# The last row norms of a hybrid encoder block: ScalarE's order up to tile 6 of the last down products is left to the scheduler, and one small tile grows to 128 bytes

## The chip, the core and the metric

The kernel runs on one core of a Trainium2 chip (trn2). The metric is device time in microseconds, the median of several executions. Times inside a profile are counted from the start of the profiled execution's span.

## What is computed

One encoder layer for 1024 frames of width 1024, all in float32. Only the last lines matter for the change, and the shape of what runs before them:

```python
h = rmsnorm(x, norm1_g)
qkv = h @ w_in                                  # 1024 x 3072
mixed = concat(rmsnorm(chunked_attention(...), norm_a_g),
               rmsnorm(stick_breaking_attention(...), norm_b_g))
x = x + mixed @ w_out
x = x + conv_gated_mlp(rmsnorm(x, norm2_g), ...)  # 1024 -> 2 x 2816 -> conv3 -> SiLU gate -> 1024
return rmsnorm(x, final_g)

def rmsnorm(x, g):
    y = x * rsqrt(mean(x * x, axis=-1) + 1e-6)
    return y * g
```

The end of the kernel computes the last part of the down projection (2816 to 1024), the residual sum, and the final norm of each frame.

## The kernel before

Data lies transposed: a tile has 128 of the 1024 features on its partitions and the 1024 frames along its free dimension, so the output is eight such tiles, here called tile 0 to tile 7 (`d` in the code). A float32 product is made of three products of rounded halves (`high` and `low` of both operands), so each product in the code is three matmuls.

The down projection takes most of the last 200 us. Twenty of the 22 blocks of 128 hidden features go through a scheme with seven products per block pair (L2391). The last two blocks are left to `last_down` (L2251), which is the kernel's end. It cuts the 1024 frames into three pieces, `LAST = ((0, 3), (3, 6), (6, 8))` in units of 128 frames, so 384, 384 and 256 frames. For each piece it goes over the eight tiles:

- TensorE forms tile d's product in six matmuls (`dnl`, L2313).
- VectorE adds it to the sum so far (L2318; into `x2n`, and for the last piece into `res`).
- ScalarE squares the result (`x2_part`, L1679 to L1689): tile 0 goes straight into an accumulator `n_acc` (L1683), the other squares into one of two buffers `n_sq` (L1688), from which GpSimd adds them into the accumulator (L1689). The last tile of the second piece and the last three of the third have accumulators of their own.
- In the last piece, and for the tiles that GpSimd will scale, ScalarE also multiplies by the norm's gain (`gain`, L2298, and L2325).

When a piece's tiles are through, `final` norms it: TensorE sums the accumulators over the partitions (`n_ms`, small matmuls, L171), ScalarE takes the square root (L163) and VectorE the reciprocal (L164), TensorE spreads the result over the partitions by transposes (`n_rb`, L184), ScalarE copies that to `n_rbs` (L2275), VectorE (L2289) and GpSimd (L2287) scale the tiles, and SP sends them out (L2292; L2280 and L2281 for the last piece). The norm of a piece is worked into the tile loop of the piece behind it (`go`): totals behind tile 2's product, transposes behind tile 3's, then a scaling between the adds. On TensorE this order is fixed for the whole kernel. So TensorE reaches the transposes of piece one after tile 3 of piece two, and must wait there if the root and the reciprocal are not done.

Before the first root, ScalarE has to load the table that holds it (ACT_TABLE_LOAD, also L163).

Who sets the order: each engine runs its queue in order. Inside a `tc.manual_schedule(engines=...)` an engine's instructions stand in the order in which the code writes them; outside it a scheduler places them at build time by its own estimate of when operands are ready. Before, `last_down` as a whole runs under a manual order for VectorE, ScalarE and GpSimd; TensorE has one throughout, and SP's order in `last_down` is left to the scheduler.

The second place that the change touches is at the kernel's start. `all_v` (L283) asks for a tile `ms` of 16 float32 values a partition, 64 bytes, for sums of squares. Tiles of a pool lie one behind another, and behind this one lies the place of the tag `c`, used by `v_c` in `all_v` and later by `a22l`, the low half of one operand in the key and query projections, which TensorE streams in the products of L1257.

Of the kernel before, what the change touches and what calls it, by code (L numbers as in the profile page):

```python
# [9 lines left out]
F32 = mybir.dt.float32  # L10
# [6 lines left out]
P = 128  # L17
T = 1024
D = 1024
KT = 8  # L20
# [47 lines left out]
def tile_hybrid_block(  # L68
# [14 lines left out]
    V, S, PE, GP = nc.vector, nc.scalar, nc.tensor, nc.gpsimd  # L83
# [20 lines left out]
    def zbank(name):  # L104
        return pools["psum"].tile([P, GW], F32, tag="z", name=name, bufs=4)
# [14 lines left out]
    def c1(off):  # L120
        t, off = (cst, off) if off < C_W0 else (taps["t"], off - C_W0)
        return t[:, off : off + 1]
# [36 lines left out]
    def cols(k):  # L159
        return slice(k * P, (k + 1) * P)  # L160
# [16 lines left out]
    def rstd(sums, c0, c1, width, rn, name):  # L177

        root(rn[:, c0:c1], totals(sums, c1 - c0, name), width)

    def across(ob, rn, c0, c1):

        for c in range(c0, c1):
            PE.transpose(ob[:, cols(c - c0)], rn[:, c : c + 1].to_broadcast([P, P]), ident)  # L184
# [14 lines left out]
    with tc.tile_pool(name="kp", bufs=2) as kp:  # L199
# [48 lines left out]
        def all_v():  # L248
# [9 lines left out]
            def area(*tiles):  # L258
                return [t[:, r] for t in tiles for r in halves]

            def own(tag, dt=F32R, shape=(P, T)):
                return pools["sbuf"].tile(list(shape), dt, tag=tag, name=f"v_{tag}", bufs=1)
# [17 lines left out]
            ]  # L280
            t4_low = []
            row = area(kp.tile([P, D], F32, tag="rb", name="row", bufs=1))
            ms = own("ms", F32, (P, 2 * KT))  # L283

            def bring(t, src, r):
                nc.sync.dma_start(t[:, r], src[:, r])
# [464 lines left out]
        flow, raw_chains = Flow(), {}  # L751
        S.preload_act_table_set("sqrt_and_others")
        right = all_v()

        fs = Ring(3)
# [397 lines left out]
        shares, pts, x2, yh, yl, yb_of, yq_of, bias_of = {}, {}, {}, {}, {}, {}, {}, {}  # L1153
# [322 lines left out]
        with stage("b"):  # L1476
# [10 lines left out]
            ending = []  # L1487
            for b in range(len(items) + 3):
# [15 lines left out]
                if ending:  # L1504
                    pair, ending = ending, []
# [21 lines left out]
                if 0 <= b - 2 < len(items):  # L1527
# [3 lines left out]
                    if (b - 2) % 4 == 3:  # L1531
                        ending = units[k & ~1 : (k | 1) + 1]
# [62 lines left out]
        for b in range(len(blocks) + 2):  # L1595
            cur = blocks[b] if b < len(blocks) else None
            turning = blocks[b - 1] if 0 <= b - 1 < len(blocks) else None
            ending = blocks[b - 2] if 0 <= b - 2 < len(blocks) else None
# [80 lines left out]
        def x2_part(x2, d, r, accs, pool, name, sq=None):  # L1679

            own = KT - len(accs)
            if d == 0 or d > own:
                S.activation(accs[max(d - own, 0)], x2[d][:, r], AF.Square)  # L1683
            else:
                if sq is None:
                    sq = pool.tile([P, GW], F32, tag="sq", name=f"{name}_sq{d}", bufs=1)
                sq = sq[:, : r.stop - r.start]
                S.activation(sq, x2[d][:, r], AF.Square)  # L1688
                GP.tensor_tensor(out=accs[0], in0=accs[0], in1=sq, op=ALU.add)  # L1689
# [67 lines left out]
    with stage("ffn"):  # L1757
# [3 lines left out]
        def at(slot, name, dt=F32):  # L1761
            pool = wp if slot == "wr" else fp if slot[0] == "s" else cp
            return pool.tile([P, T], dt, tag=slot, name=name, bufs=1)
# [418 lines left out]
        dn_p, x2n, u2n, bank = {}, [None] * KT, [], {}  # L2182
# [57 lines left out]
        NP = 10  # L2240
# [7 lines left out]
                last_w[f] = [at(where[3 + n, k], f"lw{f}_{k}", F32R) for k in (2, 3)]  # L2248
                late.append(lambda f=f: split(*last_w[f], last_raw[f][0]))

        def last_down(chunk, x2):  # L2251
            accs = [
                at(where[1 + i // 2, 2 + i % 2], f"n3_acc{i}") for i in range(4)
            ]
            res = [
                at(where[7, i], f"res{i}").rearrange("p (d t) -> p d t", d=4) for i in range(2)
            ]
            sqs = [at(where[8, i], f"n3_sq{i}") for i in range(2)]

            def final(c0, c_end):  # L2260
                sl = slice(c0 * P, c_end * P)
                last = accs[: {3: 1, 6: 2, 8: 4}[c_end]]
                if c_end == KT:
                    gain(4)
                    gain(5)
                rstd([a[:, sl] for a in last], c0, c_end, D, rn2, f"n3_{c0}")
                if c_end == KT:
                    gain(6)
                    gain(7)
                yield  # L2270
                n = (c_end - c0) * P
                ob = zbank(f"n3_{c0}_rb")[:, :n]
                across(ob, rn2, c0, c_end)
                rb = fp.tile([P, GW], F32, tag="eb", name=f"n3_{c0}_rbs", bufs=1)[:, :n]
                S.copy(rb, ob)  # L2275
                if c_end == KT:
                    for a, g in ENDS:
                        y = res[a // 4][:, a % 4 : a % 4 + 2, :]
                        f = (rb if g else ob).rearrange("p (o t) -> p o t", o=1).to_broadcast([P, 2, n])
                        (GP if g else V).tensor_tensor(out=y, in0=y, in1=f, op=ALU.mult)  # L2280
                        nc.sync.dma_start(outT[a : a + 2, :, sl].rearrange("d p t -> p d t"), y)  # L2281
                    return
                pool_d = POOL_D[c_end]
                for d in range(KT) if c_end == 6 else sorted(range(KT), key=lambda d: d not in pool_d):
                    x = y = x2[d][:, sl]
                    if d in pool_d:
                        GP.tensor_tensor(out=y, in0=x, in1=rb, op=ALU.mult)  # L2287
                    else:
                        V.scalar_tensor_tensor(  # L2289
                            out=y, in0=x, scalar=c1(C_GF + d), in1=ob, op0=ALU.mult, op1=ALU.mult  # L2290
                        )
                    nc.sync.dma_start(outT[d][:, sl], y)  # L2292
                    if d not in pool_d:
                        yield

            def gain(d):
                y = res[d // 4][:, d % 4, :]
                S.activation(y, y, AF.Copy, scale=c1(C_GF + d))  # L2298

            def go(steps):  # L2300
                for _ in range(steps):
                    while todo and next(todo[0], 1):
                        todo.pop(0)

            todo = []
            for c0, c_end in LAST:
                sl = slice(c0 * P, c_end * P)
                for d in range(KT):
                    o = (med if d % 2 else pj)(f"dnl_{d}_{c0}")[:, : (c_end - c0) * P]
                    for n, f in enumerate(chunk):  # L2310
                        (wh, wl), (xh, xl) = last_w[f], last_x[f]
                        for i, (w, t) in enumerate(((wh, xh), (wh, xl), (wl, xh))):
                            PE.matmul(  # L2313
                                o, w[:, cols(d)], t[:, sl], start=n == 0 and i == 0,
                                stop=n == len(chunk) - 1 and i == 2,
                            )
                    y = x2[d][:, sl] if c_end < KT else res[d // 4][:, d % 4, :]
                    V.tensor_tensor(out=y, in0=x2[d][:, sl], in1=o, op=ALU.add)  # L2318
                    last = accs[: {3: 1, 6: 2, 8: 4}[c_end]]
                    x2_part({d: y}, d, slice(0, y.shape[1]), [a[:, sl] for a in last], None, f"n3_{c0}", sqs[d % 2][:, :GW])  # L2320
                    if c_end == KT:
                        if d < 4:
                            gain(d)
                    elif d in POOL_D[c_end]:
                        S.activation(x2[d][:, sl], x2[d][:, sl], AF.Copy, scale=c1(C_GF + d))  # L2325
                    if c_end < KT:
                        go((d > 1) + 2 * (d == KT - 1))
                    elif d in (2, 3, 4):
                        go(1)
                todo.append(final(c0, c_end))  # L2330
            go(3)
            next(todo[-1])
            go(20)
# [74 lines left out]
            do()  # L2408
        own_order.__exit__(None, None, None)
        loads_order.__exit__(None, None, None)  # L2410
        with tc.manual_schedule(engines={V.engine, S.engine, GP.engine}):
            last_down([2 * NP, 2 * NP + 1], x2n)
    pe_order.__exit__(None, None, None)


# [61 lines left out]
```

## Time and profile before

| | |
|---|---|
| median of 3 runs | 1212.38 us (1211.32 to 1212.62) |
| the profiled execution's own time | 1212.13 us |
| its span | 1210.4 us |
| TensorE (PE) busy | 1189.5 us, 98% |
| VectorE (DVE) busy | 925.2 us, 76% |
| ScalarE (ACT) busy | 685.6 us, 57% |
| GpSimd (POOL) busy | 159.9 us, 13% |
| `last_down` begins on TensorE (first dnl matmul) | 1170.8 us |
| last dnl matmul ends | 1200.8 us |
| mean granted TensorE clock | 0.996 |

PE is TensorE's matmuls, PEld its weight loads, DVE VectorE, ACT ScalarE, POOL GpSimd, SP the engine that issues the transfers. A row of instructions gives start, duration, engine, source line, operation, output and inputs, shapes and count, and in brackets the engine's idle time before it with what ended that wait. A row in which several instructions are merged gives the time from the first one's start to the last one's end. A matmul's row lasts longer than the distance to the next, since matmuls overlap. A row of stages gives the stretch, its length, each engine's busy time with the number of instructions that touch it, the granted share of TensorE's clock, the share of the DMA engines' time and GB/s.

### The profile page before, as it was taken

What the parts mean: (1) busy time and instruction counts of PE and PEld (TensorE: products, weight loads), DVE (VectorE), ACT (ScalarE), POOL (GpSimd) and SP (SyncE); (2) the same over time, 40 slices, a digit from 0 to 9 for tenths busy, and PEclk for the clock granted to TensorE, in tenths of its full rate; (3) what the DMA queues carried; (4) which work ended last, traced back from release to release, by engine and by line L of the source; (5) the groups of instructions that cost most, each with busy time, mean ns of one, the idle gap of its engine ahead of it and who ended that gap; (6) DMA issues with size and microseconds to landing.
All of it is one profiled execution on the core that took longest, in us unless ns stands there. A gap on an engine that the chain in (4) does not pass through costs nothing.

```text
span 1210.4 us, 17073 instructions
## 1 busy us (share of the span) xinstructions
PE 1189.5 (98%) x6268; PEld 986.1 (81%) x6268; DVE 925.2 (76%) x1382; ACT 685.6 (57%) x1252; POOL 159.9 (13%) x161
## 2 busy tenths in 40 slices
PE   9999999999999999999999999999999999999996
PEld 7788888888878778788888888888888888888886
DVE  7957749888666767469997776877777779879885
ACT  7865336766667667334766555555555545444425
POOL 0001031102210111331000000000000013133044
PEclk9999999999999999999999999999999999999998
DMA  9467677777468831143122213222231294510003
GB/s 332 134 212 260 193 243 190 214 182 200 140 176 271 215 107 53 37 155 107 53 105 88 89 69 105 70 87 87 70 105 68 91 389 200 214 65 1 1 1 139
DMA packets 73793, 166.92 MB, mean 138 GB/s; under 512 B 7783, under 2 KB 23271, under 8 KB 73710
## 3 DMA queue, kind: packets, MB, share of 16 engines
q1 hardware_dynamic: 73566, 165.79, 42.7%
q8 instruction: 49, 0.80, 0.3%
q14 instruction: 34, 0.28, 0.1%
q10 hardware_dynamic: 144, 0.05, 0.0%
HBM read 118.60 MB, written 47.20 MB: 137 GB/s over the span
## 4 chain that ended last, share of the span: by engine, by line
PE 87%; DVE 7%; ACT 3%; DMA 1%; issue 1%; SPq 1%; DVEq 0%; ACTq 0%
PE u_a L1877 9%; PE u_c L1877 9%; PE u_e L1877 9%; PE dz L2391 8%; PE u_b L1877 5%; PE dj L2391 4%; PE dm L2391 4%; PE pa L154 3%; PE pb L154 3%; PE v_x L508 3%; PE k_p L154 3%; PE yb L1013 3%; PE tpb L999 3%; PE q_p L154 3%; PE yy L1146 2%; PE v_y L508 2%
## 5 line engine op out<-in xcount | busy, mean ns | idle before, releaser
L972 DVE TENSOR_TENSOR_SCAN acts<-zb,first 128x128 f32<-128x128 f32 (+7 forms) x64 | 86.5, 1351 | 18.4 <-ACT zb L981 18.4
L1901 DVE SCALAR_TENSOR_TENSOR vt<-cv,taps,vt 128x1023 f32<-128x1023 f32 (+1 forms) x44 | 58.2, 1323 | 3.3 <-ACT vt L1895 2.5
L1901 DVE SCALAR_TENSOR_TENSOR gt<-cg,taps,gt 128x1023 f32<-128x1023 f32 (+1 forms) x44 | 56.5, 1285 | 1.6 <-ACT gt L1895 0.8
L132 POOL TENSOR_TENSOR dx_0wl<-dr,dx_0wh 128x512 fp32r<-128x512 f32 x1 | 1.4, 1370 | 412.3 <-ACT dx_0wh L2144 412.3
L981 ACT ACTIVATE zb<-zb 128x128 f32<-128x128 f32 (+7 forms) x64 | 41.0, 640 | 26.3 <-PE zb L964 26.3
L1091 ACT ACTIVATE pa<-sa,sta 128x640 f32<-128x640 f32 (+4 forms) x64 | 42.7, 668 | 18.0 <-DVE sta L1082 14.6
L1895 ACT ACTIVATE gt<-cg,cst,taps 128x1024 f32<-128x1024 f32 x22 | 27.4, 1244 | 35.9 <-DVE cg L1769 35.8
L1003 ACT COPY tb<-tpb 128x128 f32<-128x128 f32 (+3 forms) x96 | 43.0, 484 | 6.1 <-PE tpb L999 5.4
L1127 ACT COPY pta<-tpa 128x512 f32<-128x512 f32 (+3 forms) x80 | 36.9, 483 | 13.3 <-PE tpa L1123 13.1
L999 PE MATMUL tpb<-ident,acts 128*128 128x128 f32 x288 | 43.2, 277 | 0.0
L1082 DVE TENSOR_REDUCE sta<-sa 128x1 f32<-128x640 f32 (+4 forms) x64 | 41.8, 655 | 1.3
L1766 DVE TENSOR_TENSOR up_r<-up_r 128x512 f32<-128x512 f32 x60 | 41.3, 688 | 0.8
L1123 PE MATMUL tpa<-ident,pa 128*128 128x128 f32 x240 | 37.9, 277 | 1.1 <-ACT pta L1127 1.1
L999 PEld LDWEIGHTS tpb<-ident,acts 128*128 128x128 f32 x288 | 33.1, 140 | 6.3 <-issue 2.6
L1079 DVE TENSOR_TENSOR sa<-sa,bias 128x256 f32<-128x256 f32 (+1 forms) x64 | 26.4, 414 | 11.0 <-PE sa L1064 7.8
L1123 PEld LDWEIGHTS tpa<-ident,pa 128*128 128x128 f32 x240 | 27.9, 140 | 8.0 <-issue 2.6
L2065 ACT COPY u_b<-u_a 128x512 f32<-128x512 f32 x19 | 10.8, 571 | 38.1 <-PE u_a L1877 38.1
L1146 PE MATMUL yy<-pta,v 128*64 128x256 f32 (+1 forms) x288 | 29.7, 349 | 0.0
L1013 PE MATMUL yb<-tb,dv 128*64 128x128 f32 x448 | 29.2, 273 | 0.0
L154 PE MATMUL pb<-yh,wo_h 128*128 128x512 f32 x64 | 26.9, 421 | 1.8 <-DVE x L1221 1.8
L1689 POOL TENSOR_TENSOR n_acc<-n_acc,n_sq 128x384 f32<-128x384 f32 (+2 forms) x23 | 24.4, 1060 | 29.7 <-ACT n_sq L1688 28.8
L154 PE MATMUL k_p<-hTh,k_h 128*128 128x512 f32 x64 | 27.6, 432 | 0.0
(1400 smaller groups left out, 4004.9 us busy)
## 6 DMA issues: line engine op xcount, KB each, us to landing
up_r<-in_w_up_dram SPq DMA_DIRECT2D x44, 512.0 KB, 3.5
act<-vt SPq DMA_DIRECT2D x22, 512.0 KB, 2.6
dr<-in_w_dn_dram SPq DMA_DIRECT2D x20, 512.0 KB, 7.4
dr<-act SPq DMA_DIRECT2D x20, 512.0 KB, 8.2
wv<-in_w_v_dram SPq DMA_DIRECT2D x16, 256.0 KB, 5.4
xin<-in_xT_dram SPq DMA_DIRECT2D x16, 256.0 KB, 5.4
row<-in_x_rows_dram SPq DMA_DIRECT2D x16, 256.0 KB, 2.6
raw<-in_w_in_dram SPq DMA_DIRECT2D x8, 512.0 KB, 5.3
```

Source lines behind the costliest of these rows:

```text
L154: PE.matmul(o, w[:, sl], t[:, rows(g)], start=first and i == 0, stop=last and i == 2,)
L508: PE.matmul(bank[j], t[:, cols(j)], w, start=p in (1, 5) and k == 0 and i == 0, stop=k == 3 and i == 2, skip_group_check=True,)
L972: V.tensor_tensor_scan(out=a[:, :w], data0=z, data1=first[:, :w], initial=1.0, op0=ALU.mult, op1=ALU.max,)
L999: PE.transpose(tp[:, cols(b)], self.a[h][:, cols(b0 + b)], ident)
L1003: mine.append(flow.add(on_s(m * P, lambda o=o, tp=tp: S.copy(o, tp))))
L1013: PE.matmul(yy[HS[h], :], (d if j else v)[:, off : off + 64], self.at[h][:, self.c0[h] + j * P : self.c0[h] + (j + 1) * P], start=j == 0, ...
L1091: on_s(w + 170, lambda: S.activation(po, full, AF.Exp, bias=st[:, h : h + 1], accum_out=st[:, 2 + h : 3 + h])),
L1123: PE.transpose(tp[:, cols(b)], self.pr[src][:, cols(c)], ident)
L1146: PE.matmul(yy[HS[h], q], v[:, c * P + h * 64 : c * P + (h + 1) * 64], t[:, h], start=j == 0, stop=j == len(parts) - 1, skip_group_check=True,
L1877: PE.matmul(o, w[:, cols(k)], t, start=start and k == 0 and i == 0, stop=k == 3 and i == 2, skip_group_check=True,)
L1901: V.scalar_tensor_tensor(out=t[:, : T - lag], in0=o[:, lag:], scalar=c1(c + ct), in1=t[:, : T - lag], op0=ALU.mult, op1=ALU.add,)
L2391: PE.matmul(o[m], w[:, cols(m)], t, start=i in (0, 1, 4, 5) and p == ps_[0] and j == 0, stop=p == ps_[-1] and j == 2, skip_group_check=True,)
```

## The change

`last_down` gets an `ExitStack`. The manual order is entered at its start for VectorE and GpSimd alone, and for ScalarE only at tile 5 of the last piece, just behind that tile's products. Up to there ScalarE's place for each instruction is the scheduler's choice; from there to the end the code's order holds again. TensorE's, VectorE's and GpSimd's written order is the same. The tile `ms` is asked for with 32 values, 128 bytes, of which the same 16 are used.

```diff
-            ms = own("ms", F32, (P, 2 * KT))
+            ms = own("ms", F32, (P, 4 * KT))[:, : 2 * KT]
...
-        def last_down(chunk, x2):
+        def last_down(chunk, x2, ending):
...
+                    if (c_end, d) == (KT, 5):
+                        ending.enter_context(tc.manual_schedule(engines={S.engine}))
                     y = x2[d][:, sl] if c_end < KT else res[d // 4][:, d % 4, :]
                     V.tensor_tensor(out=y, in0=x2[d][:, sl], in1=o, op=ALU.add)
...
-        with tc.manual_schedule(engines={V.engine, S.engine, GP.engine}):
-            last_down([2 * NP, 2 * NP + 1], x2n)
+        with ExitStack() as ending:
+            ending.enter_context(tc.manual_schedule(engines={V.engine, GP.engine}))
+            last_down([2 * NP, 2 * NP + 1], x2n, ending)
```

In the built program the tiles of tag `c` (two `v_c` and four `a22l`) lie 64 bytes further on than before, at a multiple of 128 bytes; no other tile has another address. No instruction is added or taken away, and the order on TensorE, VectorE and GpSimd is unchanged.

ScalarE around the first root, as a piece of the difference (`n3_sq0` and `n3_sq1` are the two square buffers, `x2n2` is tile 2, `n3_0` the first piece's norm):

```order
 L1688 ACTIVATE n3_sq1_10654<-x2n1_9065 128x384
-L1688 ACTIVATE n3_sq0_10653<-x2n2_9066 128x384
 L163 ACT_TABLE_LOAD
 L163 ACTIVATE rn2_78<-n3_0_ms_10764,eps_75 128x3
+L1688 ACTIVATE n3_sq0_10653<-x2n2_9066 128x384
+L2275 COPY n3_0_rbs_10784<-n3_0_rb_10780 128x384
 L1688 ACTIVATE n3_sq1_10654<-x2n3_9067 128x384
-L2275 COPY n3_0_rbs_10784<-n3_0_rb_10780 128x384
 L1688 ACTIVATE n3_sq0_10653<-x2n4_9068 128x384
```

The square of tile 2 moved behind the table load and the root, and the copy of the spread norm moved ahead of the square of tile 3.

ScalarE around the second root (`res0` holds tiles 0 to 3 of the last piece, `n3_3` is the second piece's norm; L2298 are the gains). Before:

```order
L1683 ACTIVATE n3_acc0_10647<-res0_10651 128x256
L2298 ACTIVATE res0_10651<-res0_10651,cst_66 128x256
L1688 ACTIVATE n3_sq1_10654<-res0_10651 128x256
L2298 ACTIVATE res0_10651<-res0_10651,cst_66 128x256
L1688 ACTIVATE n3_sq0_10653<-res0_10651 128x256
L2298 ACTIVATE res0_10651<-res0_10651,cst_66 128x256
L163 ACTIVATE rn2_78<-n3_3_ms_10875,eps_75 128x3
L1688 ACTIVATE n3_sq1_10654<-res0_10651 128x256
L2298 ACTIVATE res0_10651<-res0_10651,cst_66 128x256
L2275 COPY n3_3_rbs_10899<-n3_3_rb_10895 128x384
```

and now:

```order
L1683 ACTIVATE n3_acc0_10647<-res0_10651 128x256
L1688 ACTIVATE n3_sq1_10654<-res0_10651 128x256
L2298 ACTIVATE res0_10651<-res0_10651,cst_66 128x256
L1688 ACTIVATE n3_sq0_10653<-res0_10651 128x256
L2298 ACTIVATE res0_10651<-res0_10651,cst_66 128x256
L163 ACTIVATE rn2_78<-n3_3_ms_10875,eps_75 128x3
L2298 ACTIVATE res0_10651<-res0_10651,cst_66 128x256
L1688 ACTIVATE n3_sq1_10654<-res0_10651 128x256
L2275 COPY n3_3_rbs_10899<-n3_3_rb_10895 128x384
L2298 ACTIVATE res0_10651<-res0_10651,cst_66 128x256
```

Of the gains of tiles 0 to 3 each stands one place later among the squares, so that two of them instead of three stand ahead of the root, and the copy moved ahead of the last of them.

SP's output transfers of the second piece, whose order the scheduler sets:

```order
 L2292 DMA out_0_dram<-x2n1_9065 128x384
+L2292 DMA out_0_dram<-x2n2_9066 128x384
 L2292 DMA out_0_dram<-x2n6_9070 128x384
-L2292 DMA out_0_dram<-x2n7_9071 128x384
-L2292 DMA out_0_dram<-x2n2_9066 128x384
 L2292 DMA out_0_dram<-x2n3_9067 128x384
 L2292 DMA out_0_dram<-x2n4_9068 128x384
+L2292 DMA out_0_dram<-x2n7_9071 128x384
 L2292 DMA out_0_dram<-x2n5_9069 128x384
```

Tiles 6 and 7, which GpSimd scales, moved back behind tiles that VectorE scales; in the first piece tile 2, GpSimd's only one, moved behind tile 1 likewise.

## The prediction

> **What bounds the kernel now.** I read the page first, then who waited for whom on TensorE, then the last 40 us by stage, and last those stages instruction by instruction.
>
> ```profile
> PE 1189.5 (98%) x6268; PEld 986.1 (81%) x6268; DVE 925.2 (76%) x1382; ACT 685.6 (57%) x1252; POOL 159.9 (13%) x161
> PE n_rb L184 <- DVE rn L164: 3.4, 3, 1.5
> 1184.20:1185.45 1.25, 0.00 (x1) 0.01 (x1) 0.24 (x2) 0.97 (x2) 0.59 (x1) 1.00 0.00 0
> 1194.40:1195.90 1.50, 0.00 (x0) 0.00 (x0) 0.23 (x2) 1.21 (x4) 1.22 (x2) 1.00 0.00 0
> 1195.90:1203.10 7.20, 6.64 (x44) 6.56 (x44) 4.76 (x12) 4.32 (x12) 3.39 (x4) 0.76 0.28 100
> 1203.10:1210.40 7.30, 0.56 (x2) 0.17 (x2) 2.29 (x4) 0.86 (x3) 1.27 (x1) 0.50 0.76 261
> ```
>
> TensorE is busy 98% of the span, so anywhere but at the end other engines' order costs nothing. Its largest wait is in the end: three times the transposes that spread a row norm (n_rb) wait for VectorE's reciprocal, 3.4 us together. The stage rows (columns: length, then PE, PEld, DVE, ACT and POOL busy, granted clock, DMA share, GB/s) show two such stretches with TensorE at 0.00 and ScalarE at work: the norm stands in ScalarE's queue. After the second the granted clock falls.
>
> ```profile
> 1190.01:1192.16 2.15, 2.15 (x19) 1.00 0.76 272
> 1196.34:1199.75 3.41, 3.41 (x17) 0.50 0.16 58
> ```
>
> These are the down products (dnl, 256 columns) alone. One of the 19 and one of the 17 had begun before its stretch: 18 in 2.15 us are 0.119 us each, 16 in 3.41 us are 0.213. So the second wait costs more than its 1.52 us: for 3.41 us after it products run at half rate.
>
> **The first root.** ScalarE, VectorE and GpSimd around it:
>
> ```profile
> 1182.10 0.52 ACT L1688 ACTIVATE n_sq<-x2n 128x384 f32<-128x384 f32 x1 [0.58 <-DVE x2n L2318]
> 1182.29 0.73 PE L171 MATMUL n_ms<-ones,n_acc 128*128 128x2 f32 x6
> 1182.88 1.29 PE L2313 MATMUL dnl<-lx,lw 128*128 128x384 f32 x6
> 1183.08 0.52 ACT L1688 ACTIVATE n_sq<-x2n 128x384 f32<-128x384 f32 x1 [0.46 <-DVE x2n L2318]
> 1183.62 1.28 ACT L163 ACT_TABLE_LOAD   x1
> 1184.92 0.26 ACT L163 ACTIVATE rn<-n_ms,eps 128x3 f32<-128x3 f32 x1
> 1185.21 0.18 DVE L164 RECIPROCAL rn<-rn 128x3 f32<-128x3 f32 x1 [2.17 <-ACT rn L163]
> 1185.45 0.54 PE L184 MATMUL n_rb<-ident,rn 128*128 128x128 f32 x3 [1.27 <-DVE rn L164]
> 1185.92 0.53 ACT L1688 ACTIVATE n_sq<-x2n 128x384 f32<-128x384 f32 x1 [0.74 <-DVE x2n L2318]
> 1186.36 0.46 ACT L2275 COPY n_rbs<-n_rb 128x384 f32<-128x384 f32 x1
> 1186.85 0.62 DVE L2289 SCALAR_TENSOR_TENSOR x2n<-x2n,cst,n_rb 128x384 f32<-128x384 f32 x1 [1.02 <-ACT n_rbs L2275]
> 1188.69 3.22 POOL L1689 TENSOR_TENSOR n_acc<-n_acc,n_sq 128x384 f32<-128x384 f32 x3
> 1192.39 1.08 DVE L2318 TENSOR_TENSOR res<-x2n,dnl 128x256 f32<-128x256 f32 x3
> ```
>
> Before, tile 2's square (1183.08) stands ahead of the table load, and ScalarE sits idle for VectorE's add until then. Now the load follows tile 1's square: 0.54 us after its start, as it followed tile 2's, so at 1182.64 in place of 1183.62, 0.98 us earlier. The root follows 1.30 us later, at 1183.94; the totals it reads were done at 1183.02. Root, reciprocal and transposes keep their distances: transposes at 1184.47. TensorE ends tile 3 at 1182.88 + 1.29 = 1184.17, so its wait falls from 1.27 to 0.30.
>
> The copy n_rbs also passes a square (tile 3). Transposes end 0.54 later at 1185.01; the last copy of the kernel starts 0.09 after its transposes (1203.66 to 1203.75, rows further down), so this one runs from 1185.10 to 1185.56 and VectorE's first scaling starts at 1185.59, 1.26 earlier. VectorE then alternates scalings with adds that need TensorE's tiles 4 to 7, which come 0.98 earlier; I take the middle of 1.26 and 0.98, so the three adds of 1192.39 come 1.12 us earlier, at 1191.27 (either end would move the sum by 0.14).
>
> What becomes late: the two squares. Tile 2's moves from 1183.08 to 1184.20 and tile 3's to 1185.50 (behind the copy, 0.42 earlier than 1185.92). GpSimd's running sum needs both; its last three adds then end not at 1191.91 but 0.42 earlier, at 1191.49. TensorE reaches the second totals at 1192.16 - 0.98 = 1191.18 and so waits some 0.35, a new wait: totals start at about 1191.55, 0.61 earlier.
>
> **The second root.**
>
> ```profile
> 1192.16 1.40 PE L171 MATMUL n_ms<-ones,n_acc 128*128 128x2 f32 x12
> 1192.84 0.42 ACT L1683 ACTIVATE n_acc<-res 128x256 f32<-128x256 f32 x1 [0.59 <-DVE res L2318]
> 1193.42 0.96 PE L2313 MATMUL dnl<-lx,lw 128*128 128x256 f32 x6
> 1195.39 0.24 ACT L163 ACTIVATE rn<-n_ms,eps 128x3 f32<-128x3 f32 x1
> 1195.90 0.54 PE L184 MATMUL n_rb<-ident,rn 128*128 128x128 f32 x3 [1.52 <-DVE rn L164]
> 1196.25 0.42 ACT L1688 ACTIVATE n_sq<-res 128x256 f32<-128x256 f32 x1 [0.61 <-DVE res L2318]
> 1197.11 0.46 ACT L2275 COPY n_rbs<-n_rb 128x384 f32<-128x384 f32 x1
> 1197.60 0.62 DVE L2289 SCALAR_TENSOR_TENSOR x2n<-x2n,cst,n_rb 128x384 f32<-128x384 f32 x1 [1.45 <-ACT n_rbs L2275]
> 1198.14 0.41 DVE L2318 TENSOR_TENSOR res<-x2n,dnl 128x256 f32<-128x256 f32 x1
> 1200.14 0.42 DVE L2318 TENSOR_TENSOR res<-x2n,dnl 128x256 f32<-128x256 f32 x1 [0.69 <-PE dnl L2313]
> 1200.66 1.84 PE L171 MATMUL n_ms<-ones,n_acc 128*128 128x2 f32 x16
> 1199.20 0.73 POOL L1689 TENSOR_TENSOR n_acc<-n_acc,n_sq 128x256 f32<-128x256 f32 x1 [1.67 <-ACT n_sq L1688]
> ```
>
> From ScalarE's 1192.84 to the root stand six operations, 2.55 us, 0.425 each. One of them, a gain, now stands behind the root: 2.12 us. The start moves with VectorE's adds (1.12), so the root falls at 1191.72 + 2.12 = 1193.84, 1.55 us earlier. Its totals are ready 0.61 earlier than 1193.56, at 1192.95, so the new wait for GpSimd is covered by 0.9 us of ScalarE's queue. Transposes: 1194.35. TensorE's tile 3 ends 1194.38 - 0.61 = 1193.77: the wait falls from 1.52 to 0.58. The copy no longer has a gain between it and the square: 0.42 behind the square instead of 0.86, so 1.55 + 0.44 = 1.99 us earlier, and with it VectorE's scaling and the adds of tiles 4 and 5. The gains now standing later cost nothing: their first reader is the last multiplication at 1204.16, and the third root waits for totals.
>
> The adds of tiles 6 and 7 waited for half-rate products (0.69). At full rate TensorE's last product ends at 1194.35 + 0.30 + 23 x 0.119 + 0.28 = 1197.67; here 0.30 is the distance from transposes to products (1196.20 - 1195.90) and 0.28 one product's own length. Tile 7's add can then start at 1197.7, and TensorE is no longer last. The third totals wait for GpSimd's last add, which moves 1.99 with tile 4's add: 1199.93 - 1.99 = 1197.94. They start at 1198.0 instead of 1200.66.
>
> ```profile
> 1202.54 0.26 ACT L163 ACTIVATE rn<-n_ms,eps 128x2 f32<-128x2 f32 x1
> 1203.05 0.61 PE L184 MATMUL n_rb<-ident,rn 128*128 128x128 f32 x2 [0.55 <-DVE rn L164]
> 1203.75 0.37 ACT L2275 COPY n_rbs<-n_rb 128x256 f32<-128x256 f32 x1 [0.16 <-PE n_rb L184]
> 1204.16 0.69 DVE res L2280
> ```
>
> Everything behind the totals keeps its distance: 2.66 us earlier, **the tail's sum**. The output transfers (DMA share 0.76 at the end, above) go out 1.99 to 3.1 earlier, so the queue is no fuller; if they bound, only 1.99 would arrive. SP's new order puts VectorE's outputs ahead of GpSimd's, each near the time it is ready: nothing.
>
> **The wider tile.** The tiles behind it move by 64 bytes, a22l among them, which is streamed by 16 products.
>
> ```profile
> L1257 PE MATMUL ec<-th,a22l x16: 397/397/398, 112.1 to 171.5; 128*128 128x512 f32 x16
> L1257 PE MATMUL ec<-th,a22h x16: 389/389/389, 111.7 to 171.1; 128*128 128x512 f32 x16
> ```
>
> The same product takes 8 ns more from a22l. If the place is why, 16 x 8 ns = 0.13 us is won; if not, nothing, and by the same row no more than 0.13 is lost should another place suit it worse. I take 0.13, since nothing else sets a22l apart from a22h.
>
> **Sum.** 2.66 + 0.13 = 2.79; the profiled execution's own 1212.13 (span 1210.4 and 1.7 around it) becomes 1209.3. The median of the runs, 1212.38, is 0.25 above that execution; with the same offset 1209.6, and I put 1209.5, and add the same 0.2 to each time below that is made from the profiled execution.
>
> **A rule against this.** The stage row shows the clock at 0.50 after 1.50 us without a product. The Trainium skill, "TensorE: Matmul & The Clock Gate", Part 1, says the clock falls after an idle window of about 3.4 us, judged in windows that run free of the program. By its letter a 1.5 us wait would cost no clock; the trace disagrees on that, and agrees on the window (3.41 us at 0.50). By the rule's other half the same wait is caught in some executions and not in others; that is the first rival, priced below from rows.
>
> **Rivals.** (1) *Most executions of before keep the clock*, and the profiled one was unlucky; the three runs' spread of 1.3 us leaves room for it. At full rate the adds of tiles 6 and 7 would follow tile 5's at the 0.36 spacing of 1192.39, and before's third totals would wait only for GpSimd (1199.93): 0.66 earlier than shown. The change is then worth 2.79 - 0.66 = 2.1 of the median: 1210.2. Against it: the one trace there is has the clock down.
> (2) *The clock falls all the same.* Totals, the new wait for GpSimd and the remaining 0.58 still lie close together. Then the third totals start 4.76 after the transposes, as before: 1199.11, 1.55 earlier; 1212.13 - 1.55 - 0.13 + 0.2 = 1210.7. Against it: the first wait, 1.27 beside six small totals, left the clock at 1.00.
> (3) *The change does not do all it says*: the load, standing between totals and root, starts only with the totals (1183.02). The first gain is then 0.56 instead of 0.98, and some 0.3 of the sum is lost through the chain: 1212.13 - 2.5 + 0.2 = 1209.8. The trace cannot exclude it, since before the load came 0.6 after the totals.
> (4) *Slower: GpSimd's running sum becomes the bound.* Both squares it needs are now behind a root or a copy, and VectorE is denser beside it. Up to an end at 1192.4 (0.9 of cover) it costs nothing; beyond that each us is one of TensorE's, and past 1195.2 the change loses. Five operations of GpSimd (four adds and tile 2's scaling) lie between tile 3's square (done at 1186.0) and 1191.49, 1.1 each; at twice that they end at 1197.0, 4.6 past the cover: 1212.13 - 2.79 + 4.6 + 0.2 = 1214.1. Against it: beside a VectorE that was already dense these adds took 1.07 (3.22 for three).
>
> **How the numbers follow.** Forecast 0.50 (1209.5), rival 1 0.27, rival 2 0.12, rival 3 0.07, rival 4 0.04. The range 1208.7 to 1211.4 holds the first four, with 0.7 (half the runs' spread) to each side of forecast and rival 2. A change of 0.2%, 2.4 us, is about what a measurement of this kernel can tell; the line is 1209.96. I count as faster 0.8 of the forecast, a quarter of rival 1, half of rival 3 and a tenth of rival 2: 0.51. Slower is rival 4: 0.04. The rest, 0.45, is no change that can be told. The likeliest case's own range is 1208.8 to 1210.2.
>
> **What would show it.** Right: the load right behind tile 1's square; transposes' waits of about 0.3 and 0.6 for 1.27 and 1.52; clock 1.00 through the last 24 products, which take 3.1 us instead of 4.62; third totals waiting on GpSimd; a22l at 389 ns. Wrong: clock 0.50 there; a load that waits for the totals; GpSimd's adds past 1192.4; a tail as short in an execution of before whose clock holds.

## The result, and the profile after

Seventeen executions each: the changed kernel takes 1208.78 us (median; 1208.38 to 1210.97), the kernel before 1211.55 (1210.92 to 1212.87). The ratio is 0.9978, with a 95% interval of 0.9971 to 0.9986: 2.77 us faster. In both kernels some executions take about 1.1 us longer than the rest, and the change is worth as much among these (2.84 us between the medians) as among the others (2.76), taking all 106 executions of before and 50 of this order together; why they do is open. The profiled execution took 1208.78 us, 3.35 less than the one of before.

From the page of the changed kernel: busy time by engine. From its list of who waited for whom: the transposes, and a wait that the list of before does not have (columns: total us, times, longest).

```profile
PE 1188.6 (98%) x6268; PEld 984.8 (82%) x6268; DVE 928.7 (77%) x1382; ACT 685.1 (57%) x1252; POOL 158.4 (13%) x161
...
PE n_rb L184 <- DVE rn L164: 1.3, 3, 0.6
PEld n_ms L171 <- POOL n_acc L1689: 0.5, 2, 0.4
```

The transposes' waits shrank from 3.4 us to 1.3. The two waits for GpSimd are those of the weight loads ahead of the second totals, 0.19 us (the row at 1191.07 PEld below), and of the third, 0.36; the prediction had named both. The timeline of the changed kernel's end:

```profile
1181.85 0.52 ACT L1688 ACTIVATE n_sq<-x2n 128x384 f32<-128x384 f32 x1 [0.58 <-DVE x2n L2320]
1182.04 0.73 PE L171 MATMUL n_ms<-ones,n_acc 128*128 128x2 f32 x6
1182.39 1.28 ACT L163 ACT_TABLE_LOAD   x1
1183.69 0.26 ACT L163 ACTIVATE rn<-n_ms,eps 128x3 f32<-128x3 f32 x1
1184.22 0.54 PE L184 MATMUL n_rb<-ident,rn 128*128 128x128 f32 x3 [0.29 <-DVE rn L164]
1187.78 3.23 POOL L1689 TENSOR_TENSOR n_acc<-n_acc,n_sq 128x384 f32<-128x384 f32 x3
1191.03 1.07 DVE L2320 TENSOR_TENSOR res<-x2n,dnl 128x256 f32<-128x256 f32 x3
1191.07 1.41 PEld L171 LDWEIGHTS n_ms<-ones,n_acc 128*128 128x128 f32 x12 [0.19 <-POOL n_acc L1689]
1191.07 1.50 PE L171 MATMUL n_ms<-ones,n_acc 128*128 128x2 f32 x12
1191.47 0.42 ACT L1683 ACTIVATE n_acc<-res 128x256 f32<-128x256 f32 x1 [0.39 <-DVE res L2320]
1192.59 0.40 ACT L1688 ACTIVATE n_sq<-res 128x256 f32<-128x256 f32 x1
1192.90 0.49 ACT L2298 ACTIVATE res<-res,cst 128x256 f32<-128x256 f32 x1
1193.30 0.24 ACT L163 ACTIVATE rn<-n_ms,eps 128x3 f32<-128x3 f32 x1
1193.80 0.54 PE L184 MATMUL n_rb<-ident,rn 128*128 128x128 f32 x3 [0.41 <-DVE rn L164]
1194.10 3.11 PE L2313 MATMUL dnl<-lx,lw 128*128 128x256 f32 x24
1194.47 0.46 ACT L2275 COPY n_rbs<-n_rb 128x384 f32<-128x384 f32 x1
1196.57 0.74 POOL L1689 TENSOR_TENSOR n_acc<-n_acc,n_sq 128x256 f32<-128x256 f32 x1 [1.11 <-ACT n_sq L1688]
1197.36 1.95 PE L171 MATMUL n_ms<-ones,n_acc 128*128 128x2 f32 x16 [0.15 <-POOL n_acc L1689]
1199.35 0.26 ACT L163 ACTIVATE rn<-n_ms,eps 128x2 f32<-128x2 f32 x1 [0.43 <-PE n_ms L171]
```

The two executions reach this place 0.25 us apart, so I count every row from the start of the first totals: 1182.29 before, 1182.04 now. By that count the first transposes start 0.98 us earlier, the second 1.85, the third totals 3.05 (18.37 to 15.32) and the third root 2.94 (20.25 to 17.31). The table load stands right behind tile 1's square, and the waits of 1.27 and 1.52 are 0.29 and 0.41. The last 24 products took 4.62 us before and take 3.11 now. The stretch behind the second transposes (columns: length, then PE, PEld, DVE, ACT and POOL busy, granted clock, DMA share, GB/s) of the changed kernel:

```profile
1193.80:1197.21 3.41, 3.40 (x27) 3.20 (x27) 2.39 (x6) 2.16 (x7) 1.49 (x3) 1.00 0.16 58
```

The clock stays at 1.00, where it was 0.50 in the profiled execution of before.

Of the 3.35 us between the two profiled executions 3.1 lie behind the first totals. The rest, 0.25, is far ahead of the change and no part of it. In the kernel before, TensorE waited at 982 us for a copy on ScalarE (`cv`), which stood behind casts that waited for a transfer; rows of the list of waits for 975 to 990 us:

```profile
ACT dx_0ph L2144 <- DMA dr<-act: 4.9, 2, 3.3
PE dj L2391 <- ACT cv L2116: 0.5, 1, 0.5
```

The changed kernel's list has no such wait of TensorE, and a kernel with another ending (`e10_adds`, below) has it again, at 0.47 us. So it varies between executions or kernels for a reason that no run here isolates.

### The profile page after: what moved, and what is told of

Same layout as the page of the kernel before. It is cut to its first block, busy times and chain, and to the rows that moved or that the text cites. A ratio compares the mean times of both kernels' runs of the same rounds, so it can differ in the third digit from the quotient of the medians.

```text
span 1207.1 us, 17073 instructions
## 1 busy us (share of the span) xinstructions
PE 1188.6 (98%) x6268; PEld 984.8 (82%) x6268; DVE 928.7 (77%) x1382; ACT 685.1 (57%) x1252; POOL 158.4 (13%) x161
## 4 chain that ended last, share of the span: by engine, by line
PE 87%; DVE 6%; ACT 3%; DMA 2%; issue 1%; SPq 0%; POOL 0%; DVEq 0%; ACTq 0%; POOLq 0%
PE u_a L1877 9%; PE u_c L1877 9%; PE u_e L1877 9%; PE dz L2393 8%; PE u_b L1877 5%; PE dj L2393 4%; PE dm L2393 4%; PE pa L154 3%; PE pb L154 3%; PE v_x L508 3%; PE k_p L154 3%; PE yb L1013 3%; PE tpb L999 3%; PE q_p L154 3%; PE yy L1146 2%; PE v_y L508 2%
## 5 line engine op out<-in xcount | busy, mean ns | idle before, releaser
L1766 DVE TENSOR_TENSOR dr<-dr,dr 128x512 f32<-128x512 f32 x40 | 28.8, 739 | 0.0
```

The costliest lines, as they stand in the source:

```text
L1766: eng.tensor_tensor(out=out, in0=a, in1=b, op=ALU.subtract)
```

## The experiments

Gains are told against executions of the kernel before on the same chip. The chip differs between some of the experiments.

**The order without the wider tile.** `ms` keeps its 64 bytes, and `ending` is as in the change.

> The change without the wider tile: ScalarE's order alone. By the theory of the prediction with the tile worth nothing (a22l's products still took 397 ns in the changed kernel): as fast as the whole change, 2.6 to 2.8 us under before, ratio about 0.9978. If the tile matters after all, 0.1 to 0.2 us of that is missing; if the tile carried the change, no gain.

Measured: 1208.87 us against 1211.54, ratio 0.9978 [0.9969, 0.9987]; waits of 0.29 and 0.42 us. That is the whole gain of the change, as far as intervals of 1 us can tell.

**The wider tile without the order.**

```diff
-            ms = own("ms", F32, (P, 2 * KT))
+            ms = own("ms", F32, (P, 4 * KT))[:, : 2 * KT]
```

> The wider tile alone, ScalarE's order as before. The changed kernel's a22l products took 397 ns as before, so by what that trace shows: no change, ratio 0.9997 to 1.0003, a22l at 397 ns. By the prediction's term: 0.13 us faster and a22l at 389, too little to be told by the times, but told by the row.

Measured: 1211.66 against 1211.59, ratio 1.0 [0.9991, 1.0009]. In the changed kernel, which has the same tile, the products that stream a22l:

```profile
L1257 PE MATMUL ec<-th,a22l x16: 397/397/397, 112.3 to 171.7; 128*128 128x512 f32 x16
```

They take 397 ns as before. The pad brings nothing, and the 0.13 us that the prediction put down for it fell.

**Another place for the same tile.** In the kernel before, `own("c", F32, (P, GW))` is asked for right behind `own("front", ...)`. Then a22l starts, in the built program, at byte 202,112 of a partition in place of 226,752 (226,816 in the changed kernel). Other tiles lie 2 KB higher, but not `th`, the other operand of these products.

> Before, with the tag of a22l and v_c asked for early, so that a22l lies some 24 KB lower and the tiles behind it 2 KB higher. If a22l's place at the end of the memory is why its products take 397 ns: 389 here. If it is its part in the sequence (the low half, streamed behind two products with the high half): 397 again, wherever it lies.

Measured once: 1211.57 us, and from the same view of that kernel:

```profile
L1258 PE MATMUL ec<-th,a22l x16: 389/389/389, 112.4 to 171.5; 128*128 128x512 f32 x16
```

So the place does set a22l apart, but not through 64 bytes: 226,752 and 226,816 both cost 397 ns. The condition "If the place is why" holds, and the step from it to a gain by 64 bytes was wrong. Why the upper place costs 8 ns stays open; the sum, 0.13 us, is below what these timings can tell.

**Only the first root.** The tile `ms` keeps its 64 bytes, and the scheduler's stretch of ScalarE ends at tile 0 of the last piece, so only the load, the first root and the copy behind it can move.

```diff
+                    if (c_end, d) == (KT, 0):
+                        ending.enter_context(tc.manual_schedule(engines={S.engine}))
```

> Only the first root's part: tile 2's square behind table load and root, the copy ahead of tile 3's square; the second root's order as before. Queue theory: transposes' first wait 0.3 instead of 1.27, everything behind about 1.1 us earlier (between 0.98 and 1.26), second wait still near 1.5 us, ratio 0.9990 to 0.9992. Clock theory (the gain is TensorE's clock being kept through the last products, the waits themselves are hidden): no gain, because the second wait and its clock stay.

Measured: 1210.34 us, ratio 0.9988 [0.9978, 0.9997]. TensorE's rows of its timeline:

```profile
1194.38 0.54 PE L184 MATMUL n_rb<-ident,rn 128*128 128x128 f32 x3 [1.17 <-DVE rn L164]
...
1198.47 2.16 PE L171 MATMUL n_ms<-ones,n_acc 128*128 128x2 f32 x16 [0.68 <-POOL n_acc L1689]
```

First totals start at 1181.88 in this trace, so the third start 16.59 behind them. The second wait fell to 1.17, further than the 1.5 that I had expected: the root came 1.11 us earlier, and TensorE only 0.75, since its totals now waited for GpSimd.

**Only the second root.** All of ScalarE is written by hand as before, but the gain of tile d stands one square later.

```diff
+                    if (c_end, d) == (KT, 3):
+                        gain(2)
                     x2_part({d: y}, d, ...)
                     if c_end == KT:
-                        if d < 4:
-                            gain(d)
+                        if d in (1, 2):
+                            gain(d - 1)
...
+                    if (c_end, d) == (KT, 3):
+                        gain(3)
```

> Only the second root's part: each gain of tiles 0 to 3 one place later, the copy ahead of the last gain; the first root as before. Queue theory: root 0.43 earlier, copy and scaling 0.87 earlier, second wait 1.1; 0.87 us gained where before's clock had held, 1.5 where it had fallen, median about 1.0 us, ratio 0.9990 to 0.9993. Clock theory: the larger part, 1.5 us and more, ratio under 0.9988, with the clock at 1.00 through the last 24 products.

Measured: 1210.54 us, ratio 0.9988 [0.998, 0.9997]. TensorE's rows of its timeline:

```profile
1194.91 0.54 PE L184 MATMUL n_rb<-ident,rn 128*128 128x128 f32 x3 [0.78 <-DVE rn L164]
...
1198.47 1.95 PE L171 MATMUL n_ms<-ones,n_acc 128*128 128x2 f32 x16
```

First totals start at 1182.04, so the third start at 16.43. The root came 0.73 us earlier where one gain of 0.425 less in the queue was expected. ScalarE's rows of the kernel before tell why:

```profile
1192.84 0.42 ACT L1683 ACTIVATE n_acc<-res 128x256 f32<-128x256 f32 x1 [0.59 <-DVE res L2318]
1193.29 0.51 ACT L2298 ACTIVATE res<-res,cst 128x256 f32<-128x256 f32 x1
1193.70 0.40 ACT L1688 ACTIVATE n_sq<-res 128x256 f32<-128x256 f32 x1
1194.13 0.51 ACT L2298 ACTIVATE res<-res,cst 128x256 f32<-128x256 f32 x1
```

There the gain of a tile starts 0.45 and 0.43 us after the square of the same tile. In the changed kernel (rows above) the gain at 1192.90 starts 0.31 after a square of another tile. So the five operations ahead of the root take 1.83 us (1191.47 to 1193.30) and not 2.12. I name what the rows show, the other distance with the other tile; which resource makes it was not tried.

**The clock alone.** The kernel before with its order kept; TensorE is kept busy through the second wait by nine products whose result nobody reads.

```diff
+                    if (c_end, d) == (KT, 3):
+                        spare = zbank("spare")[:, : 3 * P]
+                        for _ in range(9):
+                            PE.matmul(spare, last_w[chunk[0]][0][:, cols(0)], last_x[chunk[0]][0][:, : 3 * P], start=True, stop=True)
```

> Before, with nine spare products (384 columns, result never used) on TensorE between tile 3's products of the last piece and the transposes, 1.56 us in a wait of 1.69 by issue: the wait and ScalarE's queue stay, only the clock has no reason to fall. Queue theory: executions whose clock held gain nothing, the others 0.66; median 0 to 0.3 us faster, ratio 0.9998 to 1.0000, and the upper group of before's times (1212.4 to 1212.9) is gone or moves to the lower. Clock theory: most of the change's 2.7 us, ratio under 0.9985.

Measured: 1211.30 us against 1211.54, ratio 0.9995 [0.9987, 1.0004]. TensorE's rows of its timeline:

```profile
1181.77 0.72 PE L171 MATMUL n_ms<-ones,n_acc 128*128 128x2 f32 x6
...
1193.68 1.73 PE L2320 MATMUL spare<-lx,lw 128*128 128x384 f32 x9
1195.39 0.54 PE L184 MATMUL n_rb<-ident,rn 128*128 128x128 f32 x3
1195.68 3.11 PE L2313 MATMUL dnl<-lx,lw 128*128 128x256 f32 x24
1199.47 1.95 PE L171 MATMUL n_ms<-ones,n_acc 128*128 128x2 f32 x16 [0.68 <-POOL n_acc L1689]
```

The transposes start 13.62 us after the first totals, as before (13.61), so the filler itself delays nothing. With the clock held the third totals come at 17.70 and wait for GpSimd: 0.67 earlier than the 18.37 of before. That is rival 1's price (0.66) to 0.01 us. But the median moved by 0.24 only, with an interval from 1.6 us faster to 0.5 slower, which holds 0.67 as well as nothing.

Two readings fit that: the clock falls in a part of the executions, or the interval hides the rest. The three profiled executions with the old order (before, `e1_pad`, `e8_place`) all show the fall; TensorE's row of `e1_pad`, behind a wait of 1.53:

```profile
1195.33 0.90 PE L184 MATMUL n_rb<-ident,rn 128*128 128x128 f32 x3 [1.53 <-DVE rn L164]
...
1195.88 4.12 PE L2313 MATMUL dnl<-lx,lw 128*128 128x256 f32 x24
```

There the clock fell within the wait, at 1194.75, and the third totals start 18.12 us behind the first (1181.72). So this fall cost 0.42 us against the 17.70 of the filled kernel, where that of before cost 0.67.

The traces show what decides. Between two changes of the clock lie multiples of 3.41 us, so I cut the traces into stretches of 3.41 us that end where the clock changed. Rows of before, the third for the totals alone, and of `e3_first` (columns: length, TensorE busy, clock, DMA share, GB/s):

```profile
1192.93:1196.34 3.41, 1.89 (x16) 1.00 0.30 107
1199.76:1203.17 3.41, 2.86 (x26) 1.00 0.44 160
1199.76:1203.17 3.41, 1.84 (x16) 1.00 0.44 160
...
1193.23:1196.64 3.41, 2.26 (x19) 1.00 0.00 0
```

The clock fell behind the stretch with 2.86 us of matmuls, of which 1.84 are two-column totals, and held behind the one with 2.26 us and no totals. So the totals count for little or nothing here. Without them the first stretch holds 1.40 us: 0.96 of tile 3's products and 0.44 from 1195.90 on. In the 14 traces of this case the clock fell, or stayed down, behind every such stretch with at most 1.40 us of matmuls other than these totals (1.37 in `e1_pad`, 1.29 in `e8_place`), and behind none with 1.65 or more.

Where the boundaries fall differs from trace to trace. If every place is equally likely, the order of before has a stretch of at most 1.40 us for 0.30 of the places and of at most 1.65 for 0.46, and the order of `e3_first` for 0.28 to 0.42. In the changed order no place gives less than 1.65. So by this estimate the clock falls in 0.30 to 0.46 of the executions of before, the fall is worth 0.13 to 0.31 us on average (times 0.42 to 0.67), and three falls in three profiles were a chance of 3 to 10 in a hundred.

The mean granted clock of each execution, rounded to a thousandth, agrees. Over the 89 executions of before timed beside the experiments it averages 0.99634 (standard error 0.00011). Over 92 executions of kernels whose second wait is at most 0.44 us or filled it averages 0.99699 (0.00010). One fall to 0.50 for 3.41 us of 1210 lowers it by 0.0014, so the difference of 0.00065 would be a fall in about 0.46 of the executions, give or take 0.1. That is an estimate too: it takes all of the difference to be this one fall, although the stretch at 0.50 at the kernel's end, 4.5 to 8.6 us in the profiles, weighs more in each mean. Both fit the median's 0.24. How often exactly stays open.

**All gains behind the second root.** The changed kernel's order written by hand, with the gains of tiles 0 to 3 behind the root. Against the manual order of before:

```diff
@@ final @@
                 if c_end == KT:
+                    gain(3)
                     gain(4)
                     gain(5)
...
                 S.copy(rb, ob)
+                if c_end < KT:
+                    yield
@@ last_down @@
+                    if c_end == 6 and d in (2, 3):
+                        go(1)
                     x2_part({d: y}, d, ...)
-                        if d < 4:
-                            gain(d)
...
                     elif d in (2, 3, 4):
                         go(1)
+                        if d == 2:
+                            gain(0)
+                        if d == 3:
+                            go(1)
+                            gain(1)
+                            gain(2)
```

> The changed kernel's order written out by hand, with all four gains moved behind the second root (the first just behind it, two behind the copy, the last to the gains of tiles 4 and 5), tile unchanged. Queue theory: the second root about 0.63 us earlier than in the changed kernel, transposes then bound by TensorE itself (second wait under 0.1), 0.5 to 0.6 us under the changed kernel, ratio to before 0.9972 to 0.9975. If TensorE's or GpSimd's own chain already sets the end, as it does after the changed kernel's third totals: no gain on it, 0.9978.

Measured: 1208.76 us, ratio 0.9977 [0.9968, 0.9985]: not told apart from the change, and its median short of what was expected. Rows of its timeline, PE and ACT:

```profile
1192.81 0.49 PE L184 MATMUL n_rb<-ident,rn 128*128 128x128 f32 x3
...
1193.53 0.42 ACT L1688 ACTIVATE n_sq<-res 128x256 f32<-128x256 f32 x1 [0.68 <-POOL n_acc L1689]
1193.85 0.46 ACT L2276 COPY n_rbs<-n_rb 128x384 f32<-128x384 f32 x1
...
1196.73 1.95 PE L171 MATMUL n_ms<-ones,n_acc 128*128 128x2 f32 x16 [0.56 <-POOL n_acc L1689]
```

The second wait of TensorE is gone. But ScalarE reaches tile 3's square early and sits idle for 0.68 us, and the copy of the norm stands behind it. The row names GpSimd's add, which frees the square's buffer at 1193.49; VectorE's add of tile 3, which the next expectation names, ended at 1193.43, so both held the square. Third totals start 15.10 after the first (1181.63), only 0.22 earlier than in the changed kernel, though the root came 0.70 earlier (10.56 against 11.26). The next run tests whether the bound had moved from the root to the copy.

**The copy ahead of that square.** One line of the kernel above:

```diff
-                    if c_end == 6 and d in (2, 3):
+                    if c_end == 6 and d in (2, 3) or (c_end, d) == (KT, 3):
                         go(1)
```

with the `go(1)` behind tile 3's square taken out.

> The hand-written order with the gains behind the second root, and now also the copy of the second norm ahead of tile 3's square. In the run without that the square waited for VectorE's add, the add for TensorE's tile 3, and the copy stood behind it, so the root's 0.55 us came down to 0.2 at the third totals. Theory (the copy behind the square ate it): copy and scaling 0.4 to 0.5 us earlier, third totals likewise, 0.5 us under the changed kernel, ratio to before 0.9973 to 0.9976. Rival (GpSimd's own sum sets the totals): no gain on 0.9978.

Measured: 1207.87 us, ratio 0.9971 [0.9962, 0.9981]. Rows of its timeline:

```profile
1193.36 0.48 ACT L2276 COPY n_rbs<-n_rb 128x384 f32<-128x384 f32 x1 [0.48 <-PE n_rb L184]
1193.74 0.42 ACT L1688 ACTIVATE n_sq<-res 128x256 f32<-128x256 f32 x1
...
1196.27 1.95 PE L171 MATMUL n_ms<-ones,n_acc 128*128 128x2 f32 x16
```

The copy waits only for its transposes. Third totals start at 14.60 (first totals 1181.67), 0.72 earlier than in the changed kernel and 0.50 earlier than in `e6_better`. So the place of the copy was the bound there. In medians the gain on the changed kernel is about 0.9 us, but the intervals overlap.

**The adds ahead of the scalings.** Made from `e6_better`, without the line of `e9_copy`: VectorE's adds of tiles 4 and 5 each stand ahead of a scaling, and the gains of tiles 1, 2, 5 and 7 stand later.

```diff
@@ final @@
                     gain(4)
-                    gain(5)
                 rstd([a[:, sl] for a in last], c0, c_end, D, rn2, f"n3_{c0}")
                 if c_end == KT:
+                    gain(5)
                     gain(6)
-                    gain(7)
...
                 if c_end == KT:
+                    gain(7)
                     for a, g in ENDS:
@@ last_down @@
-                    elif d in (2, 3, 4):
+                    elif d in (2, 3, 4, 5):
                         go(1)
                         if d == 2:
                             gain(0)
-                        if d == 3:
-                            go(1)
-                            gain(1)
-                            gain(2)
+                        if d > 3:
+                            gain(d - 3)
```

> The hand-written order with the gains behind the second root, and VectorE's adds of tiles 4 and 5 each ahead of the scaling that stood before it, gains 1 and 2 behind the squares of tiles 4 and 5. Theory: the third totals wait for GpSimd's add of tile 4, which waits for VectorE's add; that add comes about 0.9 us earlier, and TensorE's last product (not GpSimd) releases the totals: 0.8 us under the run with the gains moved alone, about 1207.9, ratio 0.9969 to 0.9973. Rival (the output transfers or the gains at the end take over): 0.9976 and above.

> The version with VectorE's adds ahead once more, for its time: it had five runs. Its tail, from the first totals to the third root, was 16.27 us against 17.31 in the changed kernel, so about 1.0 us under the changed kernel's 1208.8: 1207.6 to 1207.9, ratio 0.9967 to 0.9971. If the output transfers took the gain back, 0.9976 and above.

Measured: 1207.76 us against 1211.52, ratio 0.9966 [0.9954, 0.9979]; again, on another chip, 1207.51 against 1211.77, 0.9966 [0.9954, 0.9978]. Rows of the first one's timeline:

```profile
1197.19 1.85 PE L171 MATMUL n_ms<-ones,n_acc 128*128 128x2 f32 x16
...
1199.09 0.26 ACT L163 ACTIVATE rn<-n_ms,eps 128x2 f32<-128x2 f32 x1
```

Third totals start 14.37 after the first (1182.82) and the third root 16.27, which is 1.04 earlier than the changed kernel's 17.31; the second trace has 14.35 and 16.25. As expected no wait for GpSimd stands ahead of the totals any more: its last add ends at 1197.04, and TensorE's products run on to the totals. 1207.51 and 1207.76 us stand 1.0 to 1.4 below the changed kernel's medians of 1208.78 to 1208.87, and 1.9 below the one beside it (next). This is the lowest median of the versions tried, but it is not told apart from that of `e9_copy` (1207.87), and its interval against before still overlaps the changed kernel's a little.

**The changed kernel beside the others,** on two chips.

> The changed kernel itself, on the same chip and beside the same runs of before as the others of this call: ratio 0.9976 to 0.9980, second wait 0.4, a22l at 397.

> The changed kernel itself, beside the two others on the same chip: ratio 0.9976 to 0.9980.

Measured: 1208.78, ratio 0.998 [0.9971, 0.9989], and 1209.62, 0.998 [0.9972, 0.9989]. Third totals start at 15.31 in both traces, so the ending repeats to 0.01 us where it was profiled. The two profiled executions, 1208.33 and 1208.60, differ by 0.27, and that lies ahead of the first totals (1181.59 and 1181.87). Where the 0.84 between the medians arises is not shown.

## Why the prediction was right, and where its terms were not

1209.5 was predicted, 1208.78 came, near the lower end of the range and just below the likeliest case's own; a gain of 2.79 was summed, 2.77 measured. The 0.7 us between the times is the starting point: the three executions of before known then had a median of 1212.38, the seventeen have 1211.55. The mechanism is the one that was argued, but the agreement of the gain to 0.02 us is luck: three terms were off and cancel.

- **The first root** was right: 0.98 earlier, a wait of 0.29 (0.30 predicted), three adds 1.11 earlier (1.12). Rival 3 falls: the load at 1182.39 starts before the totals have ended (1182.77).
- **The new wait for GpSimd** is there, and smaller: 0.19 us by the weight loads, where some 0.35 was expected. GpSimd's three adds end 0.65 us earlier, not 0.42, and the second totals end 0.74 earlier, not 0.61. The step that put tile 3's square "0.42 earlier than 1185.92" was short: it came 0.50 earlier (1185.92 to 1185.17, by the count from the first totals). And the three adds follow GpSimd's scaling at 0.96 us (1186.82 to 1187.78) where it was 1.13 (1187.56 to 1188.69). Rival 4 did not come near: these adds took 3.23 us, as before (3.22).
- **The second root** came 1.84 earlier, not 1.55, and the wait is 0.41, not 0.58. The failed step is "six operations, 2.55 us, 0.425 each": a mean over distances that depend on what stands beside what. The five that are left take 1.83 us and not 2.12. This 0.29 also carries through copy and adds: the copy came 2.39 earlier, 1.99 predicted, of which another 0.10 is that it starts 0.32 us behind the square ahead of it and not 0.42.
- **The clock** was put into the sum in full, 0.66 us. The traces of `e5_fill` and before show that as its price in the profiled execution, 0.67. For the median, taking the last products from half rate to "full rate" at that price was too large by the estimates above, which give some 0.13 to 0.31 us; the median of `e5_fill` agrees and cannot confirm it. Rival 1 said this with 0.27; its price was right for the trace that it came from, and its condition holds for half of the executions or more by the same estimates. Rival 2 falls: the clock is 1.00 behind both waits in all four traces of this order.
- **The pad** brings nothing instead of 0.13: a22l's products took 397 ns before and after.

With the clock held on both sides the pure order is worth 17.70 - 15.32 = 2.38 us at the third totals and 2.43 in medians (1211.30 to 1208.87). The prediction's terms without the clock's 0.66 give 2.00. So the queue was undersized by 0.4, and clock and pad oversized by 0.5 to 0.7 by the estimate above. The halves add up in the traces: the first root 1.11 (17.70 - 16.59), the second 1.27 (17.70 - 16.43), together 2.38. In medians against before they are 1.20 and 1.00, whose intervals of about 1 us to each side hold that and cannot confirm it.

The step "the adds of tiles 6 and 7" was right: third totals wait for GpSimd (0.15 us in the row at 1197.36), no longer for products. And the traces of the experiments show what stood next: the copy, or VectorE's order of adds and scalings.

## What to carry to other kernels

When an engine at 98% waits at one place, look at what stands ahead of the awaited operation in the *other* engine's queue and move behind it whatever nobody waits for; here that order was worth 2.4 us, and after a move the next head of a queue can be the bound, as copy and add were here. Take the time that a queue saves from the distances between the operations that stay neighbours, not from a mean over the queue. A profile is one execution: before a fall of the clock seen in it is priced at full size, ask in how many executions the same stretch of little work would be caught.

## What the runs showed of the hardware

- On ScalarE a gain of the tile just squared starts 0.43 to 0.45 us after the start of that square; a gain or copy on another tile 0.31 to 0.32 (squares and gains of 128x256 float32). Why was not tried.
- The clock fell to 0.50, or stayed there, behind stretches of 3.41 us with at most 1.40 us of matmuls other than two-column totals, and held behind all with 1.65 or more, in the 14 traces here; 1.84 us of totals in a stretch did not keep it up. So a wait of 1.52 us was enough behind such totals. That it held behind waits of 1.17 (`e3_first`) and 1.27 us says little: where the boundaries lie decided as well. The Trainium skill, "TensorE: Matmul & The Clock Gate", Part 1, gives an idle window of about 3.4 us that runs free of the program. The stretch of 3.41 us agrees; that the window must be idle throughout does not.
- With the clock down again at its very end (from 1200.05), the sixteen last totals of `e3_first` took 2.16 us in place of 1.95.
- A product that streams a22l (128x512) takes 397 ns with the tile at byte 226,752 or 226,816 of a partition and 389 at 202,112.
